# Split-weight ring tiles at seven places modulo 256 bytes instead of one, with twelve small columns packed into one tile

## The chip, the core and the metric

One Trainium2 chip, of which the kernel uses one core. The time is the device time of one execution in microseconds (us). The kernel before takes 1808.33 us (median of two runs, 1808.29 and 1808.37). Engine names are those of the profile: PE is TensorE's matmul, PEld its weight load (the stationary operand), DVE is VectorE, ACT is ScalarE, POOL is GpSimd, SP is SyncE, which issues nearly all DMAs here.

## The reference

Two request groups of 512 tokens and 1024 features go through the same two-layer trunk: a differential-attention layer, a bidirectional retention layer, each with a residual, and a last RMSNorm. Cut to what matters:

```python
h = rms_norm(x, norm_g[0]); q, k, v, gate = split(h @ da_w_in)      # 1024 -> 4 x 2048
q, k = rotary(q) * 128 ** -0.5, rotary(k)                           # 16 half-heads of 128
p = softmax(q @ k.T)                                                # pairs of half-heads
o = rms_norm((p[even] - lam * p[odd]) @ v) * (1 - lambda_init) * silu(gate)
x = x + o @ da_w_out                                                # 2048 -> 1024
h = rms_norm(x, norm_g[1]); q, k, v, gate = split(h @ ret_w_in)     # 1024, 1024, 2048, 2048
q, k = rotate(q), rotate(k) * 128 ** -0.5                           # 8 heads of 128
o = forward_retention(q, k, v) + backward_retention(q, k, v)        # chunks with decay
x = x + (rms_norm(o) * silu(gate)) @ ret_w_out
y = rms_norm(x, final_norm_g)
```

All is float32. The kernel keeps that precision by writing each operand as a sum of two fp32r parts, a rounded high part and the rest, and multiplying three of the four pairs: high by high, high by low, low by high (`PASSES`).

## The kernel before, in words

The work is a list of operations that a planner (class `Plan`) records in program order and then arranges into one order for each engine from its own costs; the order written out is what runs. The planner knows tiles by name and by how many buffers their ring has. It does not know where a tile lies in memory.

**Projections.** The weights come in blocks of 512 rows by 256 columns, 512 KB, into four tiles `raw` (`take`, L531). `prep` (L551) adds and subtracts blocks into `st` tiles for a seven-product scheme of the Strassen kind, and splits each result: ACT copies it rounded into half of a `ws` tile or a tile of its own (`hi_of`, L400), DVE subtracts to get the rest (`lo_of`, L403). `ws` is a ring of `WS_BUFS = 7` tiles of 4096 bytes in each partition. `product` (L586) multiplies. In the "pair" form (L599) `ws` is the stationary operand, 128 columns at a time, and the activations `Bop`, split tiles in the arena or in pool `cp` (`b` in the profile), move, 512 columns at a time. In the "wide" form (L609) it is the other way: `Bop` is stationary and 256 columns of `ws` move. The results go through tiles `c`, `e`, `m`, `os` to DRAM.

**Attention** (layer 1). For each head, group and 128 tokens: scores (L1116), exponentials (ACT, L1134), the combination of two half-heads (L1150), a transpose (L1161), the product with v (L1181), and between them the output projection (`out_step`, L871): its matmul, L891, has the arena tile `oT` as stationary operand and 512 columns of a `ws` tile moving, and DVE adds the result to x (L896). **Retention** (layer 2) has scores (L1315), states (L1339), the products near (L1359) and far (L1367), and the same `out_step`. `square` (L912) and `x_norm` (L1012) keep sums of squares in columns `ssf`, a ring of twelve tiles of one float32 each.

**Where tiles lie.** Every tile is made when it is first used, by `view` (L280), and tiles of a pool lie one behind the other in that order: first pool `sm` with the small ones (32 bytes each at least), then `cp`, the arena, then `wk` with `raw`, `ws`, `os`, `st`, `m`, `e`, `c`. All large tiles are multiples of 256 bytes long, so within a pool they keep one place modulo 256. The arena is cut by hand: `slot` (L303) puts a tile at `32 + at * 1024 + shift` floats. The last tile, `e_7`, ends 32 bytes short of the 229,376 bytes of a partition.

In the text, "place" is an operand's byte address in the partition modulo 256. It follows from the sizes alone:

| matmul line | stationary operand, place | moving operand, place |
|---|---|---|
| L599 pair projections | `ws`, 224 | `Bop`, 32 |
| L609 wide projections | `Bop`, 32 | `ws`, 224 |
| L891 output projections | `oT`, 160 | `ws`, 224 |
| L1116 scores | q, 32 | k, 96 |
| L1181 product with v | v, 96 | weights `aT`, 32 |
| L1315 retention scores | k, 160 | q, 96 |
| L1339 states | k, 96 | v, 32 |
| L1359, L1367 retention products | v or state, 32 | scores or q, 96 |
| L1028, L1161 transposes | x or p, 32 | identity, 32 |
| L1010 warm-up | zeros, 224 | zeros, 224 |

`raw`, `st`, `m`, `e`, `c` and `os` lie at 224 as well.

Of the kernel before, what the change touches and what calls it, by code (L numbers as in the profile page):

```python
# [9 lines left out]
F32 = mybir.dt.float32  # L10
# [5 lines left out]
P = 128  # L16
# [237 lines left out]
def trunk_kernel(  # L254
# [12 lines left out]
    sm = ctx.enter_context(tc.tile_pool(name="sm", bufs=1))  # L267
    cp = ctx.enter_context(tc.tile_pool(name="cp", bufs=1))
    ar = ctx.enter_context(tc.tile_pool(name="ar", bufs=1))
    wk = ctx.enter_context(tc.tile_pool(name="wk", bufs=1))  # L270
# [6 lines left out]
    places = {}  # L277
    cnt = [0]

    def view(pool, tag, i, size, shape, dt=F32):  # L280


        if size % 16 and pool in (cp, wk):
            pool = sm
        if (tag, i) not in places:
            places[tag, i] = pool.tile([P, size], F32, tag=f"{tag}{i}", name=f"{tag}_{i}", bufs=1)
        n = math.prod(shape[1:])
        t = places[tag, i][0:shape[0], 0:n]
        if dt != F32:
            t = t.bitcast(dt)  # L290
        if len(shape) == 3:
            t = t.rearrange("p (a b) -> p a b", a=shape[1])
        elif len(shape) == 4:
            t = t.rearrange("p (a b c) -> p a b c", a=shape[1], b=shape[2])
        return t

    def work(tag, shape, bufs, dt=F32, name=None):
        size = SIZE.get(tag, shape[1])
        return Buf(plan, tag, bufs, lambda i: view(wk, tag, i, size, shape, dt))
# [24 lines left out]
    def const(shape, tag, dt=F32, size=None):  # L324
        return Buf(plan, tag, 1, lambda i: view(cp, tag, i, size or math.prod(shape[1:]), shape, dt))
# [27 lines left out]
    def bank(tag, name=None):  # L353
        return Buf(plan, tag, BUFS[tag], lambda i: view(pj if tag == "pj" else sc, tag, i, S, [P, S]))
# [1098 lines left out]
    for i in range(N2 + 1):  # L1453
        if i < N2:
# [9 lines left out]
            if i == N2 - 1:  # L1464
                for n in range(2):
                    f = fin_ps[n] = bank("sc", "fin")
# [67 lines left out]
```

## Time and profile before

| what | value |
|---|---|
| median of the runs | 1808.33 us |
| span of the profiled execution | 1807.0 us, 1.3 us under the median of the runs |
| PE busy | 1794.9 us, 99% of the span, 10299 matmul records |
| PEld busy (beside PE) | 1558.1 us, 86% |
| DVE, ACT, POOL busy | 1477.1 us (82%), 895.1 us (50%), 169.5 us (9%) |
| mean DMA rate | 182 GB/s |

The profiled execution has no time of its own beside its span; what lies around the span is the 1.3 us to the median of the runs. A busy PE is not PE at its peak: the ends of matmuls are modelled, and one begins before the record of the one before has ended. What a matmul takes from the next is read from the chain that ended last, where a piece such as "8.24 ... x36" is the time in which 36 matmuls began one after another.

### The profile page before, as it was taken

The numbers are of one execution on the slowest core, as the hardware profiler recorded it, in microseconds if no ns is written. First come the engines' busy times: TensorE is split into PE (matmuls) and PEld (weight loads), VectorE is DVE, ScalarE is ACT, GpSimd is POOL, SyncE is SP. The second block draws the span as 40 slices with busy tenths as digits, with TensorE's granted clock in tenths as the row PEclk, the third lists the DMA queues.
The fourth block names the chain that finished last, engine by engine and source line by source line (L and its number), as shares of the span: only waits on it lengthen the run. The fifth ranks groups of instructions, "written<-read, shape, count | busy, mean of one in ns | idle before, by whom it ended". The sixth has DMA issues, their size and how long they took to land.

```text
span 1807.0 us, 27780 instructions
## 1 busy us (share of the span) xinstructions
PE 1794.9 (99%) x10299; PEld 1558.1 (86%) x10299; DVE 1477.1 (82%) x2319; ACT 895.1 (50%) x1856; POOL 169.5 (9%) x323
## 2 busy tenths in 40 slices
PE   9999999999999999999999999999999999999998
PEld 6789889898988888888888888898989898888887
DVE  7958787778699888888888897787887967888887
ACT  7753444433434565554555866444434355444346
POOL 1000000000000022222322300000000000111113
PEclk9999999999999999999999999999999999999999
DMA  6444455555545685444554524464657559765662
GB/s 217 134 126 137 161 140 178 184 168 155 174 126 175 201 334 198 178 156 159 190 204 140 190 73 146 140 210 146 205 156 228 151 170 396 272 238 182 225 218 94
DMA packets 162767, 328.81 MB, mean 182 GB/s; under 512 B 12724, under 2 KB 76872, under 8 KB 162632
## 3 DMA queue, kind: packets, MB, share of 16 engines
q1 hardware_dynamic: 162304, 326.71, 54.1%
q8 instruction: 81, 1.33, 0.3%
q14 instruction: 54, 0.44, 0.1%
q10 hardware_dynamic: 328, 0.34, 0.1%
HBM read 209.55 MB, written 117.44 MB: 181 GB/s over the span
## 4 chain that ended last, share of the span: by engine, by line
PE 93%; DVE 2%; DMA 2%; ACT 2%; issue 1%; POOL 0%; SPq 0%; POOLq 0%; DVEq 0%; ACTq 0%
PE pj L599 20%; PE pj L891 19%; PE sc L599 10%; PE pj L609 10%; PE o L599 8%; PE o L1181 5%; PE sc L1116 5%; PE sc L609 5%; PE o L609 2%; PE o L1359 2%; PE tp L1161 2%; PE sc L1315 1%; PE o L1367 1%; PE tp L1339 1%; DMA raw<-in_ret_w_out_dram 1%
## 5 line engine op out<-in xcount | busy, mean ns | idle before, releaser
L891 PE MATMUL pj<-ws,arena 128*128 128x512 f32 x1542 | 391.2, 397 | 0.0
L891 PEld LDWEIGHTS pj<-ws,arena 128*128 128x128 f32 x1542 | 277.7, 188 | 52.7
L599 PE MATMUL pj<-b,ws 128*128 128x512 f32 x1080 | 265.0, 392 | 0.0
L599 PEld LDWEIGHTS pj<-b,ws 128*128 128x128 f32 x1080 | 201.4, 188 | 43.0
L403 DVE TENSOR_TENSOR ws<-st,ws 128x512 fp32r<-128x512 f32 (+1 forms) x192 | 147.9, 774 | 74.8 <-ACT ws L400 56.7
L896 DVE SCALAR_TENSOR_TENSOR b<-pj,crr,b 128x512 f32<-128x512 f32 (+1 forms) x257 | 189.9, 744 | 21.4 <-PE pj L891 21.0
L403 DVE TENSOR_TENSOR ws<-raw,ws 128x512 fp32r<-128x512 f32 (+1 forms) x164 | 141.5, 868 | 71.3 <-ACT ws L400 61.0
L400 ACT CAST ws<-st 128x512 fp32r<-128x512 f32 (+1 forms) x192 | 132.4, 693 | 121.4 <-PE pj L599 36.4
L599 PE MATMUL sc<-arena,ws 128*128 128x512 f32 x768 | 186.8, 392 | 0.0
L599 PE MATMUL o<-arena,ws 128*128 128x512 f32 x744 | 180.0, 393 | 1.1 <-ACT m L385 0.6
L599 PEld LDWEIGHTS sc<-arena,ws 128*128 128x128 f32 x768 | 144.0, 188 | 31.3
L400 ACT CAST ws<-raw 128x512 fp32r<-128x512 f32 (+1 forms) x164 | 125.7, 772 | 87.0 <-PE o L599 45.0
L599 PEld LDWEIGHTS o<-arena,ws 128*128 128x128 f32 x744 | 138.4, 188 | 31.7 <-DVE arena L463 1.4
L599 PE MATMUL pj<-arena,ws 128*128 128x512 f32 x648 | 160.3, 392 | 0.4 <-DVE arena L463 0.4
L599 PEld LDWEIGHTS pj<-arena,ws 128*128 128x128 f32 x648 | 120.8, 188 | 26.7 <-DVE arena L463 0.7
L1134 ACT ACTIVATE b<-sc,nm 128x512 f32<-128x512 f32 x128 | 88.0, 689 | 66.9 <-DVE nm L1124 66.5
L636 ACT COPY c<-pj 128x512 f32<-128x512 f32 x104 | 60.9, 586 | 119.7 <-PE pj L599 66.4
L609 PE MATMUL pj<-ws,b 128*128 128x256 f32 x960 | 116.8, 276 | 0.0
L609 PEld LDWEIGHTS pj<-ws,b 128*128 128x128 f32 x960 | 113.2, 188 | 0.7
L1116 PE MATMUL sc<-arena 128*128 128x512 f32 x384 | 101.2, 395 | 0.3 <-ACT b L1134 0.3
L1181 PEld LDWEIGHTS o<-arena 128*128 128x128 f32 x768 | 93.1, 188 | 2.7
L1181 PE MATMUL o<-arena 128*128 128x256 f32 x768 | 93.7, 278 | 0.0
(207 smaller groups left out, 2855.9 us busy)
## 6 DMA issues: line engine op xcount, KB each, us to landing
qk<-os SPq DMA_DIRECT2D x192, 256.0 KB, 3.6
arena<-qk SPq DMA_DIRECT2D x96, 512.0 KB, 5.8
raw<-in_da_w_in_dram SPq DMA_DIRECT2D x64, 512.0 KB, 5.1
v<-os SPq DMA_DIRECT2D x64, 512.0 KB, 4.3
arena<-v SPq DMA_DIRECT2D x64, 512.0 KB, 4.1
raw<-in_ret_w_in_dram SPq DMA_DIRECT2D x48, 512.0 KB, 4.8
os<-g SPq DMA_DIRECT2D x32, 512.0 KB, 7.4
g<-e SPq DMA_DIRECT2D x48, 256.0 KB, 4.6
```

The lines of the kernel that those rows point to most:

```text
L400: act(n, lambda: nc.scalar.copy(dst(), src()), r, w)
L403: dve(n, lambda: nc.vector.tensor_tensor(dst(), src(), hi().bitcast(F32), op=ALU.subtract), r, w)
L599: nc.tensor.matmul(ps.t, a[u][0]()[:, k, :], bt[k][:, v, :], start=(opens and k == 0 and i == 0), stop=(k == 3 and i == 2), skip_group_che ...
L609: nc.tensor.matmul(ps[:, (t % 2) * 256:(t % 2) * 256 + 256], bt[k][:, v, t * P:(t + 1) * P], a[u][0]()[:, k, :], start=(opens and t % 2 == ...
L636: act(S, lambda c=c, ps=ps: nc.scalar.copy(c.t, ps.t), [ps], [c])
L891: nc.tensor.matmul(ps[:, here], o[a][:, e, t * P:(t + 1) * P], u[b][:, e, here], start=(m == 0), stop=(m == 5))
L896: axpy(n, lambda half=half, here=here, ps=ps: nc.vector.scalar_tensor_tensor(half, ps[:, here], rr[:, t % 2:t % 2 + 1], half, op0=ALU.mult ...
L1116: nc.tensor.matmul(s.t, q[:, a, t * P:(t + 1) * P], k[:, b, :], start=(n == 0), stop=(n == 2))
L1134: act(840, lambda j=j, s=s, m=m: nc.scalar.activation(p[:, j, :], s.t, AF.Exp, bias=m.t, accum_out=sm[:, 2 * j + n:2 * j + n + 1]), [s, m] ...
L1161: nc.tensor.transpose(tp[:, j * P:(j + 1) * P], p[:, 0, j * P:(j + 1) * P], ident.t)
L1181: nc.tensor.matmul(o[:, e * 256:(e + 1) * 256], v[b][:, j, e * P:(e + 1) * P], aT[a][:, j, :], start=(n == 0), stop=(n % 12 == 11), skip_g ...
L1359: nc.tensor.matmul(o[:, e * 256:(e + 1) * 256], v_[v][:, 2 * c + j, e * P:(e + 1) * P], a_[:, u, j * 256:(j + 1) * 256], start=(e == 0 and ...
```

## The change: where tiles begin

Six tiles of 32 bytes, `gap1` to `gap6`, that nothing reads or writes are made just ahead of the ring tiles `ws_1` to `ws_6`. The twelve `ssf` columns become twelve neighbouring floats of one tile of 128 bytes; before, each took 32 bytes.

```diff
         if size % 16 and pool in (cp, wk):
             pool = sm
+            if tag == "ssf":
+                if tag not in places:
+                    places[tag] = sm.tile([P, 16 + 16], F32, tag=tag, name=tag, bufs=1)
+                return places[tag][:, i:i + 1]
+        if tag == "ws" and i and (tag, i) not in places:
+            places["gap", i] = wk.tile([P, 8], F32, tag=f"gap{i}", name=f"gap_{i}", bufs=1)
         if (tag, i) not in places:
             places[tag, i] = pool.tile([P, size], F32, tag=f"{tag}{i}", name=f"{tag}_{i}", bufs=1)
```

Pool `sm` becomes 12 x 32 - 128 = 256 bytes shorter, so whatever lies between it and `ws_1` keeps its place modulo 256: `Bop`, the identity, all arena tiles, the four `raw` tiles, `ws_0`. Behind it, each gap moves all later tiles by 32 bytes:

| tiles | place before | place after |
|---|---|---|
| `ws_0` ... `ws_6` | 224 for all | 224, 0, 32, 64, 96, 128, 160 |
| `os_0`, `os_1`, `os_2` | 224 | 0, 0, 160 |
| `st_0`, `st_1`, `st_2` | 224 | 32, 32, 160 |
| `m_0` ... `m_3` | 224 | 224, 32, 32, 64 |
| `c_0` ... `c_3` | 224 | 128, 128, 160, 160 |
| `e_0` ... `e_7` | 224 | 224, 96, 128, 160, 160, 160, 160, 160 |

Both programs hold the same instructions on every engine, in the same order and with the same waits; only addresses differ.

## Prediction

> **What bounds the kernel now.** I read the page's span, its engines' busy time and the chain that ended last; then who waits for the ring tiles; then how often, and how fast, a matmul reads one.
>
> ```profile
> span 1807.0 us, 27780 instructions
> PE 1794.9 (99%) x10299; PEld 1558.1 (86%) x10299; DVE 1477.1 (82%) x2319; ACT 895.1 (50%) x1856; POOL 169.5 (9%) x323
> ...
> PE 93%; DVE 2%; DMA 2%; ACT 2%; issue 1%; POOL 0%; SPq 0%; POOLq 0%; DVEq 0%; ACTq 0%
> PE pj L599 20%; PE pj L891 19%; PE sc L599 10%; PE pj L609 10%; PE o L599 8%; PE o L1181 5%; PE sc L1116 5%; PE sc L609 5%; PE o L609 2%; PE o L1359 2%; PE tp L1161 2%; PE sc L1315 1%; PE o L1367 1%; PE tp L1339 1%; DMA raw<-in_ret_w_out_dram 1%
> ```
>
> TensorE is the bound: it is busy 99% of the span and 93% of the chain. So the time follows from how long one matmul holds the next one back, times their number. From the answer about tile `ws`, under the DVE split that fills it (L403), the one row of who on TensorE waited for it:
>
> ```profile
>   PEld o L599: 0.2, 1
> ```
>
> One weight load waited, 0.2 us. The splits are ahead of TensorE, so what happens to ACT and DVE at the ring costs nothing until it eats that lead. The matmuls that read the ring, from the groups by form (first number: busy us; second: mean ns of the modelled record, not the interval):
>
> ```profile
> L891 PE MATMUL pj<-ws,arena 128*128 128x512 f32 x1530 | 389.8, 398 | 0.0
> L599 PE MATMUL pj<-b,ws 128*128 128x512 f32 x1080 | 265.0, 392 | 0.0
> L599 PE MATMUL sc<-arena,ws 128*128 128x512 f32 x768 | 186.8, 392 | 0.0
> L599 PE MATMUL o<-arena,ws 128*128 128x512 f32 x744 | 180.0, 393 | 1.1 <-ACT m L385 0.6 <-DVE arena L463 0.3
> L599 PE MATMUL pj<-arena,ws 128*128 128x512 f32 x648 | 160.3, 392 | 0.4 <-DVE arena L463 0.4
> L609 PE MATMUL pj<-ws,b 128*128 128x256 f32 x960 | 116.8, 276 | 0.0
> L609 PE MATMUL sc<-ws,arena 128*128 128x256 f32 x768 | 89.6, 276 | 0.0
> L609 PE MATMUL pj<-ws,arena 128*128 128x256 f32 x576 | 73.1, 277 | 0.0
> L609 PE MATMUL o<-ws,arena 128*128 128x256 f32 x384 | 45.0, 277 | 0.0
> L599 PE MATMUL sc<-b,ws 128*128 128x512 f32 x120 | 29.1, 391 | 0.0
> ```
>
> That is 3360 at L599 and 1530 at L891, 512 columns each, and 2688 at L609 of 256 columns: 7578 in all. Their intervals, from the chain in order of time (start, us, what):
>
> ```profile
> 75.27 8.24 PE pj L599 x36
> ...
> 174.49 5.44 PE pj L609 x48
> 179.93 5.44 PE sc L609 x48
> 185.37 5.44 PE pj L609 x48
> 190.81 2.75 PE pj L599 x12
> ...
> 199.02 2.75 PE o L599 x12
> ...
> 1783.58 13.76 PE pj L891 x60
> ```
>
> 8.24 / 36 = 229 ns at L599, 13.76 / 60 = 229 ns at L891, 5.44 / 48 = 113 ns at L609. So 4890 x 0.229 + 2688 x 0.1133 = 1120 + 305 = 1425 us, 79% of the span, is intervals of matmuls that read the ring. One nanosecond on each is 7.6 us, or 0.4%.
>
> **The change part by part.** No instruction, wait or order changes, so every effect has to be a duration that depends on an address.
>
> *TensorE, the ring as operand.* During a matmul the next stationary tile is loaded. Before, the two reads that run together begin 64 bytes apart modulo 256 in all three lines (224 against 32, 32 against 224, 160 against 224). After, the seven tiles are at distances of every multiple of 32, zero among them: `ws_2` and `Bop` both at 32, `ws_6` and `oT` both at 160. The trace has some of these distances already, where one line follows another. The piece at 185.37 ends in a wide projection that moves `ws` at 224 while the first stationary `ws`, also at 224, is loaded for the L599 piece at 190.81: distance zero. The piece at 174.49 ends beside a load at distance 64. Both take 5.44 us for 48 intervals. The piece at 190.81 ends with `Bop` at 32 moving and `Bop` at 32 loading, the one at 199.02 with `ws` at 224 loading beside `Bop` at 32: both 2.75 us for 12. So one meeting of equal places costs no more than the rounding of a row, 10 ns, and these rows show 0. If each matmul at equal places cost those 10 ns, that is one tile in seven: 7578 / 7 x 0.010 = 11 us. Distances of 32, 96, 160 and 224 occur nowhere in the trace: every matmul operand of before sits on 32 modulo 64, and `ws_1`, `ws_3`, `ws_5` leave it. For these I have only the spread that line and tile bring among matmuls of one shape. Chain of the retention stage:
>
> ```profile
> 1548.65 0.69 PE tp L1339 x6
> 1549.35 0.71 PE sc L1315 x6
> ...
> 1551.43 1.36 PE o L1359 x12
> 1552.79 0.68 PE o L1367 x6
> ```
>
> 115, 118, 113 and 113 ns for 256 columns. L1315 and L1339 have the sign of distance that L609 has (stationary 64 above moving, modulo 256) and L609 runs at 113, so the 5 ns do not follow the distance. I take 0 for TensorE, the value of the nearest rows, the meetings at distance zero. The upper end is 5 ns on 256 columns and, in proportion, 10 ns on 512, on six tiles of seven: 6/7 x (4890 x 0.010 + 2688 x 0.005) = 42 + 12 = 54 us. The lower end comes from plain float32 matmuls at the warm-up:
>
> ```profile
> 8.78 2.31 PE L1010 MATMUL sc<-e 128*128 128x512 f32 x5
> ...
> L1010 PE MATMUL sc<-e x16: 592/592/1220, 1.4 to 10.9; 128*128 128x512 f32 x16
> ```
>
> Less the last record's 0.592 us, four intervals take 1.72 us, 430 ns each. If such a record streams its 512 columns twice, an estimate, one pass is 215 ns, 14 ns under the 229 of the split matmuls; in proportion 256 columns would be 107, 6 ns under 113. If the places of before caused that and the six moved tiles lost it all: 6/7 x (4890 x 0.014 + 2688 x 0.006) = 59 + 14 = 73 us of gain.
>
> *ACT and DVE, the ring as output.* Rows of both engines on tiles at different places (arena outputs at 32, 96 and 160, `ws` and `os` at 224):
>
> ```profile
> L403 DVE TENSOR_TENSOR ws<-st,ws 128x512 fp32r<-128x512 f32 x160 | 108.9, 685 | 56.7 <-ACT ws L400 56.2
> L403 DVE TENSOR_TENSOR arena<-tp,arena 128x512 fp32r<-128x512 f32 x64 | 43.8, 685 | 4.9 <-ACT arena L400 4.4
> L403 DVE TENSOR_TENSOR arena<-e,arena 128x512 fp32r<-128x512 f32 x36 | 24.4, 683 | 1.3 <-ACT arena L400 1.1
> ...
> L400 ACT CAST ws<-st 128x512 fp32r<-128x512 f32 x160 | 98.7, 621 | 74.9 <-PE pj L599 30.3 <-issue 13.1 <-PE sc L599 11.1
> L400 ACT CAST arena<-e 128x512 fp32r<-128x512 f32 x36 | 22.4, 622 | 28.6 <-DVE e L1322 27.4 <-DVE e L463 1.1
> ```
>
> 685, 685, 683 and 621, 622 ns: place does not show. I take 0; it hides behind TensorE, and without cover the 2 ns between these rows on the 356 splits of `ws` would be 0.7 us.
>
> *DMA.* `os` tiles are stored from other places; the page has their landing:
>
> ```profile
> qk<-os SPq DMA_DIRECT2D x192, 256.0 KB, 3.6
> ```
>
> DMA is 2% of the chain, half of it the load of `raw` that the chain names, and `raw` keeps its place. I take 0; the other half, 1% or 18 us, is what the transfers of moved tiles can hold at most, and 5% more on it would be 0.9 us.
>
> *The packed columns.* The instructions that write and read `ssf` stay; only their start addresses come 4 bytes apart:
>
> ```profile
> L917 ACT ACTIVATE ssf<-ssf,ssf x17: 278/294/322, 1006.7 to 1801.4; 128x1 f32<-128x1 f32 x17
> ```
>
> I take 0, as for the other rows of ACT; their whole spread, 322 - 278 = 44 ns, on all 17 would be 0.7 us.
>
> Sum: 1807.0 + 0 = 1807.0 us of span, and the 1.3 us to the median of the runs: **1808.3 us**.
>
> **The rivals.**
>
> *Unaligned neighbours slow TensorE.* Two reads of memory that begin at equal places, or off the common 32 modulo 64, hold each other up for part of every load. For it: the spread from 113 to 118 shows that identical work can take 4% longer with other tiles. Against it: the equal places above cost nothing. Price: 5 ns on each of 6/7 x 7578 = 6495 matmuls, 32 us: 1841 us; with the 10 ns at 512 columns 1862 us. It counts as slower from 36 us, 5.6 ns for each matmul on a moved tile. The Trainium skill, page "SBUF — State Buffer", section "Who interferes with whom", says that PE has two independent read ports, for the moving operand and for the load, and never waits on anyone; by that this rival's time would be the forecast's, and the intervals at equal places agree.
>
> *The old place was the bad one.* The 14 ns between 229 and 215 are the mark of a collision at a distance of 64 that the spread removes for most distances. Price: up to 73 us, 1735 us; half of it, 1772 us, where some distances stay bad. Against it: L1367, where no ring tile takes part, runs at the same 113 as L609, and the distance-zero meetings are not shorter. The Trainium skill, page "TensorE: Matmul & The Clock Gate", section "Wait — 56ns, not 53.3ns?", gives 215.7 ns between warm matmuls of 512 columns; by that page something holds up the split matmuls by 13 ns, which the row of 229 shows too but does not tie to a place.
>
> *The change does nothing that time can see*, for lack of any such sensitivity at all: that is the forecast's own case.
>
> **How the numbers follow.** Forecast, within 0.8% of before: 0.62. Slower rival: 0.24, of which 0.15 beyond 2%. Faster rival: 0.14, of which 0.07 beyond 2%. About 2% is what a measurement of this kernel can tell from no change. So faster 0.07, within 0.62 + 0.09 + 0.07 = 0.78, slower 0.15. The range takes in the slower rival's 1841 us, to 1845, and below a third of the faster one's 73 us, to 1785; what lies outside is the upper price of the first and the fuller gains of the second, about 0.2 together.
>
> **What would show it.** Right: pieces of 36 at L599 take 8.24 us again, of 48 at L609 5.44, of 60 at L891 13.76, and mean records stay at 392, 276 and 398 ns. The slower rival: pieces of 12 at L599 longer than 2.75 us by amounts that return every seventh tile, 2.81 or more, and all other lines unchanged. The faster one: pieces nearer 2.6 us. If DVE rows at L403 leave 685 ns, or loads begin to wait for `ws`, the cost of ACT and DVE was misjudged. The forecast is wrong above all if an odd multiple of 32 bytes matters, the distance that no row of before has.

## The result: 1.5% slower, and the profile after

The changed kernel takes 1835.12 us (1834.79 to 1835.45) against 1808.33 us: a ratio of 1.0148, 95% interval [1.0119, 1.0178]. Its page begins:

```profile
span 1833.5 us, 27780 instructions
## 1 busy us (share of the span) xinstructions
PE 1820.8 (99%) x10299; PEld 1572.8 (86%) x10299; DVE 1479.0 (81%) x2319; ACT 895.1 (49%) x1856; POOL 170.1 (9%) x323
...
PE 93%; DMA 3%; DVE 2%; ACT 1%; issue 0%; POOL 0%; SPq 0%; POOLq 0%; DVEq 0%
```

The span grew by 26.5 us and PE's busy time by 25.9 us, with the same 10299 matmuls. PE's share of the chain is 93% as before. So matmuls themselves take longer. Lines of the changed kernel carry numbers 6 higher: L605 was L599, L615 was L609, L897 was L891, L1365 was L1359. Groups by form (busy us, mean ns):

```profile
L897 PE MATMUL pj<-ws,arena 128*128 128x512 f32 x1530 | 392.2, 399 | 0.0
L605 PE MATMUL pj<-b,ws 128*128 128x512 f32 x1080 | 267.5, 394 | 0.0
L605 PE MATMUL o<-arena,ws 128*128 128x512 f32 x744 | 182.5, 396 | 1.1 <-ACT m L391 0.6 <-DVE arena L469 0.3
L615 PE MATMUL pj<-ws,b 128*128 128x256 f32 x960 | 121.9, 281 | 0.0
L615 PE MATMUL o<-ws,arena 128*128 128x256 f32 x384 | 46.9, 282 | 0.0
L1365 PE MATMUL o<-arena 128*128 128x256 f32 x384 | 49.9, 279 | 0.0
```

Over all their groups, L609's 2688 matmuls cost 13.5 us more (5 ns each), L599's 3360 cost 8.8 us (2.6 ns), L891's 1530 cost 2.4 us (1.6 ns). Some 2 us more fell on retention and score matmuls that no ring tile touches, such as L1359 (276 to 279 ns). The chain in order of time, at the place that the prediction showed:

```profile
164.91 5.75 PE o L615 x48
...
187.79 5.65 PE pj L615 x48
193.44 2.80 PE pj L605 x12
...
202.05 2.80 PE o L605 x12
204.85 2.73 PE sc L605 x12
207.58 2.79 PE pj L605 x12
```

48 wide matmuls take 5.65 to 5.75 us here, and up to 5.81 elsewhere on the chain, where they took 5.44. Of the pair products, most take 2.80 us where they took 2.75, but one takes 2.73, and so does every seventh one behind it (the next begins at 224.29 us). By the order of the ring this is `ws_2`, the tile at 32, the same place as `Bop`; the trace does not number the tiles, so this is inferred here, and the run with all tiles at 32 below bears it out. Equal places are not the trouble in the pair form; they are its best case. ACT and DVE did not move:

```profile
L409 DVE TENSOR_TENSOR ws<-st,ws 128x512 fp32r<-128x512 f32 x160 | 109.1, 686 | 59.1 <-ACT ws L406 58.5
L406 ACT CAST ws<-st 128x512 fp32r<-128x512 f32 x160 | 98.6, 621 | 80.4 <-PE pj L605 27.3 <-issue 13.6 <-PE sc L605 11.8
```

685 and 621 ns were the means before.

### The profile page after: what moved, and what is told of

It is laid out like the page before. It is cut to its first block, busy times and chain, and to the rows that moved or that the text cites. A ratio compares the mean times of both kernels' runs of the same rounds, so it can differ in the third digit from the quotient of the medians.

```text
span 1833.5 us, 27780 instructions
## 1 busy us (share of the span) xinstructions
PE 1820.8 (99%) x10299; PEld 1572.8 (86%) x10299; DVE 1479.0 (81%) x2319; ACT 895.1 (49%) x1856; POOL 170.1 (9%) x323
## 4 chain that ended last, share of the span: by engine, by line
PE 93%; DMA 3%; DVE 2%; ACT 1%; issue 0%; POOL 0%; SPq 0%; POOLq 0%; DVEq 0%
PE pj L605 20%; PE pj L897 19%; PE sc L605 10%; PE pj L615 10%; PE o L605 8%; PE sc L615 5%; PE o L1187 5%; PE sc L1122 5%; PE o L615 2%; PE o L1365 2%; PE tp L1167 2%; PE o L1373 1%; PE tp L1345 1%; PE sc L1321 1%; DMA raw<-in_ret_w_out_dram 1%; DMA raw<-in_da_w_in_dram 1%
## 5 line engine op out<-in xcount | busy, mean ns | idle before, releaser
L897 PE MATMUL pj<-ws,arena 128*128 128x512 f32 x1542 | 393.7, 398 | 0.0
L897 PEld LDWEIGHTS pj<-ws,arena 128*128 128x128 f32 x1542 | 277.7, 188 | 54.4
L605 PE MATMUL pj<-b,ws 128*128 128x512 f32 x1080 | 267.5, 394 | 0.0
L605 PEld LDWEIGHTS pj<-b,ws 128*128 128x128 f32 x1080 | 201.5, 188 | 45.2
L605 PE MATMUL sc<-arena,ws 128*128 128x512 f32 x768 | 188.7, 394 | 0.0
L605 PE MATMUL o<-arena,ws 128*128 128x512 f32 x744 | 182.5, 396 | 1.1 <-ACT m L391 0.6
L605 PEld LDWEIGHTS sc<-arena,ws 128*128 128x128 f32 x768 | 144.0, 188 | 33.0
L605 PEld LDWEIGHTS o<-arena,ws 128*128 128x128 f32 x744 | 138.4, 188 | 34.3 <-DVE arena L469 1.4
L605 PE MATMUL pj<-arena,ws 128*128 128x512 f32 x648 | 162.0, 394 | 0.3 <-DVE arena L469 0.3
L605 PEld LDWEIGHTS pj<-arena,ws 128*128 128x128 f32 x648 | 121.0, 188 | 28.4 <-DVE arena L469 0.6
L615 PE MATMUL pj<-ws,b 128*128 128x256 f32 x960 | 121.9, 281 | 0.0
L615 PEld LDWEIGHTS pj<-ws,b 128*128 128x128 f32 x960 | 118.0, 189 | 0.6
```

The source lines that it names most:

```text
L605: nc.tensor.matmul(ps.t, a[u][0]()[:, k, :], bt[k][:, v, :], start=(opens and k == 0 and i == 0), stop=(k == 3 and i == 2), skip_group_che ...
L615: nc.tensor.matmul(ps[:, (t % 2) * 256:(t % 2) * 256 + 256], bt[k][:, v, t * P:(t + 1) * P], a[u][0]()[:, k, :], start=(opens and t % 2 == ...
L897: nc.tensor.matmul(ps[:, here], o[a][:, e, t * P:(t + 1) * P], u[b][:, e, here], start=(m == 0), stop=(m == 5))
```

## The experiments

In what follows a distance is the place of the stationary operand less that of the moving one, modulo 256. Before: 192 in L599 and L891, 64 in L609. Each ratio is to runs of the kernel before on the same chip, whose medians are 1808.6 to 1809.0 us.

### Packed columns without gaps

```diff
-        if tag == "ws" and i and (tag, i) not in places:
-            places["gap", i] = wk.tile([P, 8], F32, tag=f"gap{i}", name=f"gap_{i}", bufs=1)
```

> The packed columns alone, no gaps: all seven ring tiles at 224 again, and all tiles 256 bytes lower than before. If places modulo 256 are what counts (both theories), 1808 us, L599 at 229 ns and L609 at 113 to 114 ns. If the packing or the shift by 256 bytes bears part of the loss (the retention lines L1359 and L1367, which no ring tile touches, rose by 2 to 3 ns in the changed kernel), these two stay at 116 to 118 ns and the time is 1810 us or more.

1808.61 us, ratio 1.0003 [0.9992, 1.0015]. The retention line is back at its old mean:

```profile
L1363 PE MATMUL o<-arena 128*128 128x256 f32 x384 | 48.8, 276 | 0.0
```

The packing and the shift by 256 bytes cost nothing that shows; the loss comes with the gaps.

### All seven at 32, at 160, at 0

One gap ahead of `ws_0` alone, so that the ring has one place again; of 64 bytes in the first run (shown), of 192 and 32 bytes in the others:

```diff
-        if tag == "ws" and i and (tag, i) not in places:
-            places["gap", i] = wk.tile([P, 8], F32, tag=f"gap{i}", name=f"gap_{i}", bufs=1)
+        if (tag, i) == ("ws", 0) and (tag, i) not in places:
+            places["gap", i] = wk.tile([P, 16], F32, tag=f"gap{i}", name=f"gap_{i}", bufs=1)
```

> All seven ring tiles at 32, the place of the activations Bop: distance zero in L599 and L609. Theory A, distance (the interval follows from the distance between the two operands modulo 256, as the seven tiles of the changed kernel show it at L599: 227 ns at zero, 229 at 192, 232 at 128, 233 to 234 elsewhere): L599 at 227 ns, 6 us less than before; L609 as its tile at 32 in the changed kernel, 118 ns, 12 us more; 1813 us. Theory B, mixing (L609 and L891 lose because the high part and the rest of a weight lie at different places, so the place changes from one matmul to the next): L609 back at 113 to 114 ns, L599 at 227; 1803 us. My forecast's slower rival would have equal places cost: L599 above 229.

> All seven at 160, on 32 modulo 64 like every operand of before, distance 128 in L599. Theory A: L599 232 ns (10 us more), L609 119 ns (14 us more), 1832 us. Theory B with the place effect of L599 alone: L599 232, L609 113 to 114, 1818 us.

> All seven at 0, off 32 modulo 64. Theory A: L599 233 to 234 ns (14 us more), L609 119 ns (14 us more), L891 2 ns more (3 us), 1839 us. Theory B: L599 233 to 234, L609 113 to 114, 1823 us.

1827.38 us (1.0102 [1.0073, 1.0131]), 1838.02 us (1.0161 [1.0131, 1.0190]) and 1841.56 us (1.0181 [1.0151, 1.0210]). With every tile at 32, from the groups by form:

```profile
L605 PE MATMUL pj<-b,ws 128*128 128x512 f32 x1080 | 263.1, 390 | 0.0
L615 PE MATMUL pj<-ws,b 128*128 128x256 f32 x960 | 123.0, 283 | 0.0
```

and from its chain in order of time:

```profile
187.37 5.76 PE pj L615 x48
193.13 2.75 PE pj L605 x12
```

The pair form gains 2 ns a matmul, the wide form loses 7: 5.76 / 48 = 120 ns. So mixing places is not the cause: without any mixing, L609 is worse than in the changed kernel. Each time the wide form lost, at 118 to 120 ns. Theory A was too low by 14, 6 and 3 us in the three, theory B by 24, 20 and 19. The place 160 is on the old grid of 32 modulo 64 and still costs 1.6%.

### The same distances at other places

The first run puts a pad of 32 bytes ahead of everything, as shown. In the second the pad is of 192 bytes and a gap of 64 bytes lies ahead of `ws_0`, so that the ring stays at 224, `Bop` moves to 224 and `oT` to 96. Both runs have the packed columns and no other gaps:

```diff
     sm = ctx.enter_context(tc.tile_pool(name="sm", bufs=1))
+    sm.tile([P, 8], F32, tag="pad", name="pad", bufs=1)
```

> Packed columns, no gaps, and everything in memory 32 bytes higher: all distances as before, but every matmul operand at 0 modulo 64. Theory A: 1808 us, L599 229 ns, L609 113 to 114. Rival, alignment (being off 32 modulo 64 is what costs): L599 233, L609 118 and the retention lines 118, 1836 us or more.

> The distances of the run with all tiles at 32 (zero in L599 and L609, 128 in L891), but with the ring at its old place 224 and activations and arena moved by 192 to meet it. Theory A: that run again, 1827 us, L599 227 ns, L609 120. Rival, the ring's own place (224 is good whatever it meets): L599 229, L609 113 to 114, 1808 us.

1810.29 us (1.0009 [0.9998, 1.0020]) and 1827.87 us (1.0102 [1.0073, 1.0131]). Groups of the first, then of the second:

```profile
L604 PE MATMUL pj<-b,ws 128*128 128x512 f32 x1080 | 264.9, 392 | 0.0
L614 PE MATMUL pj<-ws,b 128*128 128x256 f32 x960 | 116.8, 276 | 0.0
```

```profile
L606 PE MATMUL pj<-b,ws 128*128 128x512 f32 x1080 | 263.1, 390 | 0.0
L616 PE MATMUL pj<-ws,b 128*128 128x256 f32 x960 | 123.0, 283 | 0.0
```

With all matmul operands off 32 modulo 64, nothing is lost that the interval can tell from zero. With the ring at its good old place but zero distance, the run with all at 32 comes back to the last digit of these rows. It is the distance, not the place, and not the alignment to 64 bytes.

### The other tiles moved, the ring left alone

```diff
+        if tag == "ws" and (tag, i) not in places:
+            for n in range(WS_BUFS):
+                places[tag, n] = wk.tile([P, size], F32, tag=f"{tag}{n}", name=f"{tag}_{n}", bufs=1)
+            places["gap", i] = wk.tile([P, 16], F32, tag="gap", name="gap", bufs=1)
```

> The ring made in one piece at 224 and everything behind it (os, st, m, c, e but the first) moved to 32. Theory A: no matmul operand changes its distance, 1808 us. Rival, writers: if the places of what ACT, DVE and the DMAs read and write bear part of the loss, 1812 us or more.

1809.07 us, 1.0001 [0.9990, 1.0012]. Moving the tiles that ACT, DVE and the DMAs use behind the ring costs nothing that shows.

### The distance by itself

A kernel of matmuls alone: weights and activations of the two forms, the weights read at a growing offset (cut to the loop, with comments added).

```diff
+        for off in [0] + ups + ups[::-1]:        # floats
+            for _ in range(4):
+                pair(off)                        # 12 matmuls of 512 columns, as L599
+            for t in range(8):
+                wide(off, t % 4)                 # 12 matmuls of 256 columns, as L609
```

> None of the reference is computed: zeros aside, the outputs are copies of the inputs, and TensorE runs split matmuls alone, in turns of 48 of the L599 kind and 96 of the L609 kind, with the weights moved against the activations by 0, 16, 32, 48, 64, 96, 128, 160, 192, 208, 224, 240, 256, 288, 320 and 448 bytes, first upward, then downward. Theory A, distance modulo 256: the L599 kind takes 227 ns at 0 and 256, 229 at 192 and 448, 232 at 128, 233 to 234 at 32, 64, 96, 224, 288 and 320; the L609 kind 113 at 192 and 448, 118 to 120 elsewhere; the same upward and downward. Rival, history: the interval hangs on how a turn is entered (L1359 ran at 113 or 118 ns with unchanged operands), so that upward and downward differ at one distance. Rival, other engines take part: alone on the chip all turns run at 227 and 113.

The chain in order of time (L282 is the pair form, L290 the wide one), for shifts of the weights of 0, 16, 32, 128, 192 and 256 bytes upward, and 16 downward:

```profile
39.04 10.91 PE one L282 x48
49.94 11.51 PE two L290 x96
61.45 11.20 PE one L282 x48
72.66 11.40 PE two L290 x96
...
95.25 11.21 PE two L290 x96
...
174.26 11.15 PE one L282 x48
185.41 11.52 PE two L290 x96
...
219.39 10.99 PE one L282 x48
230.38 10.91 PE two L290 x96
...
308.61 10.92 PE one L282 x48
319.54 11.51 PE two L290 x96
...
722.95 11.20 PE two L290 x96
```

In the pair form the weights are stationary, so the shift is the distance; in the wide form they move, so a shift of 192 is the distance 64. Divided by 48 and 96, for all shifts (two numbers where upward and downward differ by more than 0.5 ns):

| weights shifted by, bytes | pair, 512 columns, ns | wide, 256 columns, ns |
|---|---|---|
| 0, 256 | 227 | 120 |
| 16 | 233 | 119 / 117 |
| 32, 288 | 233 | 117 |
| 48 | 233 | 118 |
| 64, 320 | 233 | 118 |
| 96 | 234 | 120 |
| 128 | 232 / 233 | 120 |
| 160 | 233 | 117 / 119 |
| 192, 448 | 229 | 113.6 |
| 208 | 232 | 119 |
| 224 | 233 | 118 |
| 240 | 228 | 117 |

TensorE alone, with no other engine at work, gives the kernel's numbers: 227 and 120 at equal places, 229 and 113 at the old ones, and the pattern repeats after 256 bytes (256, 288, 320 and 448 are like 0, 32, 64 and 192). The kernel before stood at the one shift of these where the wide form is fast. The few entries that differ by direction show that distance is not quite all.

### Plain float32

```diff
-        w = sb.tile([P, 2048 + 128], F32R, tag="w", name="w")
-        b = sb.tile([P, 4096], F32R, tag="b", name="b")
+        w = sb.tile([P, 2048 + 128], F32, tag="w", name="w")
+        b = sb.tile([P, 4096], F32, tag="b", name="b")
```

> The sweep of distances 0 to 224 in steps of 32, upward, with plain float32 operands, which TensorE streams at half the columns per time or less; none of the reference is computed. If the loss is two reads at full fp32r rate getting in each other's way, the interval is the same at all distances to within 1 ns. Rival, a cost for each load whatever the rate: the spread of 7 ns stays.

The turns are half as long as in the sweep, 24 and 48 matmuls, and the shifts only go upward. Behind the first turn, which holds the start, every turn is the same, whatever the distance. From the chain in order of time:

```profile
58.86 20.60 PE one L282 x48
79.46 20.72 PE two L290 x96
100.18 20.60 PE one L282 x48
...
348.10 20.60 PE one L282 x48
368.70 20.72 PE two L290 x96
```

A record of 512 columns takes 429 ns, one of 256 takes 216 (the trace has two records for each of these matmuls, so `x48` is 24 of them). With plain float32 no distance shows.

### Spare room in the ring tiles, and oT moved

Since pair matmuls are fastest at distance 0 and wide ones at 64, the ring tiles get spare room, and the pair form reads at another offset in it. More small columns are packed to pay for it (first run; the second adds the change of `oT`, the third makes that change alone to the kernel before):

```diff
+        extra, lead = 0, 0
+        if tag == "ws":
+            extra = (16, 48)[i % 2]
+            lead = ((0, 16), (48, 0))[i % 2][len(shape) == 4]
...
-        t = places[tag, i][0:shape[0], 0:n]
+        t = places[tag, i][0:shape[0], lead:lead + n]
...
-        return [slot(16 + 2 * g + a, [P, 2, S], F32R, 32) for a in range(2)]
+        return [slot(16 + 2 * g + a, [P, 2, S], F32R, 48) for a in range(2)]
```

> Ring tiles with 64 or 192 bytes to spare, so that the pair form reads its weights at distance 0 from Bop (L599) while the wide form and the output projection keep the distances of before (64 in L609, 192 in L891); more small columns are packed to make room. Theory A: L599 227 instead of 229 ns on 3360 matmuls, 5 us as in the run with all tiles at 32, L609 113 to 114, 1803 us, ratio 0.997. Rival, history: the retention lines or L891 are entered less well and take the 5 us back, 1808 us or more.

> The same, and oT 64 bytes higher, at distance 0 from the moving weights of L891. Theory A: L891 227 instead of 229 ns on 1530 matmuls, 3 to 4 us more gained, 1799 to 1800 us. Rival, history: L891 stands in turns of 6 between other lines, so a steady interval is not reached, and the lines behind it (L1359, L1367, L1181) are entered otherwise and rise to 118 ns; 1803 us or more.

> The kernel before with oT alone 64 bytes higher: L891 at distance 0, all else as before. Theory A: 1804 to 1805 us. Rival, history: 1808 us or more, with L1359 and L1367 at 117 to 118 ns.

1813.85 us (1.0024 [1.0015, 1.0033]), 1817.85 us (1.0046 [1.0033, 1.0058]) and 1812.88 us (1.0020 [1.0012, 1.0029]): all three slower than before. Groups of the first:

```profile
L608 PE MATMUL pj<-b,ws 128*128 128x512 f32 x1080 | 262.9, 390 | 0.0
L618 PE MATMUL pj<-ws,b 128*128 128x256 f32 x960 | 120.9, 281 | 0.0
```

and a piece of its chain:

```profile
184.42 5.65 PE pj L618 x48
```

The pair form gained as meant, 6.7 us over all its groups. But the wide form, whose distance is 64 as before, runs at 5.65 / 48 = 118 ns, not 113, and lost 10.7 us. In the third, L1359, whose operands were not touched, does the same:

```profile
L1359 PE MATMUL o<-arena 128*128 128x256 f32 x384 | 50.3, 280 | 0.0
```

280 ns against 276. L891 itself, now at distance 0, gained 0.6 us where 3 to 4 were expected, and L1359, L1181, L1367, L1339 and L1116, none of them touched, lost 4.7 us together. So a line can take one of two values at an unchanged distance, and theory A has no room for that. That the turn ahead decides between them is what the next two runs test.

### How a turn is entered

The kernel of matmuls alone again, and the ring with spare room with one change: the pair product just ahead of a wide turn is read at the old distance.

```diff
+        for _ in range(2):
+            for to in (48, 16, 32):              # floats
+                turn([48] * 4, to)               # four pair products, then the wide turn
+                turn([0] * 4, to)
+                turn([0] * 3 + [48], to)
+                turn([16] * 4, to)
```

```diff
-                v.prep(p)
+                v.prep(p, ready + 1 < len(order) and order[ready + 1][0].wide)
```

> TensorE alone again, none of the reference computed. After a first turn of each kind at 192, four turns of 48 (L599 kind) and 96 (L609 kind): the wide turn always with the weights moved by 192 (the distance of L609 in the kernel before), the pair turn ahead of it at 192; at 0; three products at 0 and the last at 192; at 16. Then the same four ahead of wide turns at 64 and at 128; all twice. If the distance alone sets the interval, all four wide turns at 192 take 113.3 ns each, 10.9 us. If a turn keeps the state in which it is entered, the one after a pair turn at 0 takes 117.7 ns, 11.3 us, and the one whose last pair product is at 192 takes 10.9 us again.

> The kernel with spare room in the ring tiles, and the one pair product ahead of each turn of wide products read at the old distance 192 (24 of 280 products). If a turn keeps the state of its entry, L609 returns to 113 to 114 ns, L599 stays near 227 to 228, 6 us less than before: 1803 us, ratio 0.997. If the 118 ns of L609 in that kernel come from something else in its layout, L609 stays at 118 and the time at 1813 to 1814 us.

The wide turns at a shift of 192 in the first round, behind pair turns at 192, at 0, at 0 with the last at 192, and at 64 bytes (`turn([16] * 4, ...)` counts floats; the expectation's "16" is that), then the first of the second round:

```profile
49.70 10.91 PE two L290 x96
...
71.50 11.31 PE two L290 x96
...
93.72 11.31 PE two L290 x96
...
116.22 10.89 PE two L290 x96
...
306.55 11.00 PE one L282 x48
317.55 11.31 PE two L290 x96
```

The same 96 matmuls at one distance take 113.5 or 117.8 ns each, and keep the value for the whole turn. A pair turn at 0 leaves them slow. One product at 192 does not mend it, against my expectation, and in the second round even four do not: there a wide turn of 11.52 us stands ahead of them, and the slow state came through a pair turn at 192. That is no full rule, for in the sweep a pair turn at 192 behind a slow wide turn (11.26 us at 208.13) led into the fast one at 230.38. A pair turn shifted by 64 bytes mends it both times. At the other two shifts all four entries gave one value, 11.31 and 11.52 us.

In the kernel, the one product helped in part: 1808.11 us, ratio 0.9987 [0.9978, 0.9997] to the kernel before. Its group:

```profile
L618 PE MATMUL pj<-ws,b 128*128 128x256 f32 x960 | 118.3, 278 | 0.0
```

and three pieces of its chain:

```profile
153.71 5.66 PE pj L618 x48
...
183.95 5.44 PE pj L618 x48
...
307.13 5.65 PE pj L618 x48
```

Of the wide turns on this chain, the first takes 5.66 us for 48, those at 162 to 198 us and those from 1178 us on take 5.44 to 5.47, those at 287 to 488 us take 5.65 or 5.66: whole stretches keep one state, and the mean of 278 lies between 276 and 281. This is the fastest version found, by 0.1%; the 6 us of the expectation were not reached, since L599's gain of 6.1 us was paid back by 4.5 us on L609.

## Why the prediction was wrong, point by point

**What bounds the kernel**: right. TensorE's intervals are the time: PE's busy time holds 25.9 of the 26.5 us. The count of 7578 matmuls on the ring, 0.4% for each nanosecond, carries the result: 13.5 + 8.8 + 2.4 us are theirs.

**ACT, DVE, DMA, packed columns, each at 0**: right, shown by the run that moves the other tiles alone, by the one with packed columns alone, and by the splits into the moved ring tiles (686 and 621 ns).

**"I take 0 for TensorE, the value of the nearest rows, the meetings at distance zero"**: this step failed. The term put at 0 measured 24.7 us on the lines that read the ring. I priced a distance by one interval where two lines meet. A single meeting shows only how a turn begins; the cost sets in within a few matmuls and then stays: in the sweep at distance 0, the starts of the records in the wide turn at 49.94 us are 114 ns apart, then 119, and from the third on 120. In steady turns distance 0 is the best for 512 columns (227 ns) and among the worst for 256 (120 ns), so the rows I read could not even give the sign. The trace of before held a hint:

```profile
193.55 5.47 PE pj L609 x48
```

This turn stands behind a pair turn and takes 0.03 us more than the 5.44 of those behind a wide turn; its first five intervals are 116 to 122 ns, and only then 113. What a meeting costs shows in the turn behind it, and there I did not look.

**"So the 5 ns do not follow the distance"**: wrong as well. I compared L1315 and L1339 with L609, all at 64, and took their spread for noise of line and tile. The experiments give L609 113 and 118 ns at that one distance, so the spread cannot rule the distance out. By the starts of its records in the turn at 1548.65 us, L1339 goes from 121 to 113 and 114 ns within its six, while L1315 behind it stays at 117 and 118. That these are the same two states is likely but not shown: L1315's median interval is 116 to 118 ns in every run.

**The upper end**: 5 ns on 256 columns was the right size (measured 5, 13.5 us against 12). The 10 ns in proportion on 512 was four to six times too large.

**"About 2% is what a measurement of this kernel can tell"**: too wide. Two runs of the changed kernel gave an interval of 0.6%, [1.0119, 1.0178].

**The slower rival**, two reads that hold each other up: it is the nearest to what the runs bear out, a matmul interval that hangs on how its two operands lie to each other. That its 1841 us came near the 1835 is partly luck: it charged 5 ns to all three lines, which measured 5.0, 2.6 and 1.6. The range held the result only because this rival's price was in it. Its condition was wrong: "equal places, or off the common 32 modulo 64" is refuted by the pair form's gain at equal places, by the loss at 160 and by the run 32 bytes higher. An odd multiple of 32 bytes, the danger that the prediction named last, does cost as a distance (233 ns in the sweep at 32), but an even one such as 128 costs 232. The Trainium skill, page "TensorE: Matmul & The Clock Gate", section "Step-by-step: what each phase is for", says that loading the next tile's weights does not steal read bandwidth from the running matmul. Plain float32 agrees (429 ns at every distance). For fp32r the interval follows how the two operands lie to each other (227 to 234 ns, 113 to 120), for which that sentence has no room, and there the measurement decides.

**The faster rival**: its place was wrong. The old distance is the good one for L609. A small gain was there for L599, 2 ns, and the kernel with spare room collected it, to lose it at the entry of L609. No distance tried brought a steady turn of 512 columns below 227 ns, so 12 of the 14 ns to the estimated 215 are not the mark of any of these places.

**What was not foreseen**: some 2 us on matmuls that the change does not touch; the median interval of L1359 and L1367 went from 113 to 117 ns. That the turns ahead of them changed the state in which they are entered is argued from the kernel of matmuls alone, not shown line by line.

What stays open: which part of TensorE's read path holds the two states, and what a turn hands to the next. That load and moving operand meet in the same part of memory is argued from the period of 256 bytes and from plain float32; no run shows it.

## What to carry to other kernels

When TensorE is the bound with fp32r operands, give stationary and moving operands a fixed distance modulo 256 bytes, sweep it in a kernel of matmuls alone with the kernel's own shapes and order of passes, and keep it the same for all tiles of a ring. Then measure the whole kernel: of four layouts that the sweep made look better, three came out slower. Price such an effect from long steady turns, never from one interval at a seam. When room is made in front of tiles, or a tile is added, compare the places of matmul operands before and after.

## What the runs showed of the hardware

- The interval of fp32r matmuls depends on the distance of their two operands modulo 256 bytes: 227 to 234 ns for 512 columns, 113 to 120 ns for 256, with no other engine at work. Plain float32 shows none of it, 429 and 216 ns a record.
- At one and the same distance a turn can run in either of two states (113.5 or 117.8 ns), set by what ran ahead of it and kept, in the kernel, for 240 matmuls in a row.
